# A two-block network on one core: the state space preparation moved behind the first mixer, its product turned, records on the SyncE queue, query weights split ahead, bias tables last

## The chip, the cores and the metric

The kernel runs on one core of one Trainium2 chip, as one launch. A core has five engines with instruction streams of their own: TensorE (PE; its weight loads are PEld), VectorE (DVE), ScalarE (ACT), GpSimd (POOL) and SyncE (SP, which here only issues DMAs). The metric is the device time of one execution in microseconds, as the median of several runs; lower is better.

## The reference

Two blocks for 256 tokens of width 1024, everything in fp32. The first block has two layers, each a hybrid mixer (gated linear attention, a short convolution and latent attention side by side, then an output projection) and cross-attention to a memory of 256 tokens. The second block has two layers of half-FFN, mixer, half-FFN; its first mixer is a state space layer (S5), its second a native sparse attention (NSA).

```python
x = first_block(x, mem, ...)                 # 2 x (hybrid mixer, memory cross-attention), final norm
for layer in range(2):                       # second block
    h = h + 0.5 * _swiglu(_rmsnorm(h, ffn1_norm[layer]), ffn1_w_in[layer], ffn1_w_out[layer])
    u = _rmsnorm(h, mix_norm[layer])
    h = h + (_s5_mixer(u, ...) if layer == 0 else _nsa_mixer(u, kv, w_qg, q_norm, w_o, rel_bias))
    h = h + 0.5 * _swiglu(_rmsnorm(h, ffn2_norm[layer]), ffn2_w_in[layer], ffn2_w_out[layer])
    if layer == 0:
        kv = _shared_kv(h, ...)              # keys and values of the three branches of NSA
```

The state space layer turns its parameters into a diagonal recurrence, which does not depend on the activations:

```python
def _s5_mixer(u, a_re, a_im, log_dt, b_re, b_im, c_re, c_im, d_skip, w_glu):
    dt = jnp.exp(log_dt)[:, None]
    ab_re, ab_im = exp(a_re * dt) * cos(a_im * dt), exp(a_re * dt) * sin(a_im * dt)
    bb = (ab - 1) / a * b                    # complex, per group, state and channel
    x = associative_scan(x[t] = ab * x[t - 1] + bb @ u[t])
    y = gelu(re(c @ x) + d_skip * u)
    return y * sigmoid(y @ w_glu)
```

NSA projects queries and gates from one weight matrix, takes relative position biases from a small table, and mixes compressed, selected and window attention.

## The kernel before, in words

Activations stay in SBUF. Every large product is made of three matmuls with 12-bit halves (`mm3` and the matmul helper, line 72): `xh*hi`, `xl*hi`, `xh*lo`. Each chunk of weights (1024 rows by 256 columns, 1 MB) is loaded by SyncE (line 143) into a ring of raw buffers; ScalarE rounds it to `hi` (line 155), VectorE subtracts to get `lo` (line 156), and PE uses both. One such chunk costs PE 48 matmuls for 256 tokens.

The stages in their order on the chip, with their times from the trace: mixer 0 (about 20 to 154 us), the memory keys and output projection of layer 0 (to 188), cross-attention 0 (to 245), mixer 1 (to 374), output projection 1 (to 410), cross-attention 1 (to 450), first half-FFN (to 661), S5 with its gate (to 750), half-FFN (to 945), shared keys and values (to 980), half-FFN (to 1187), NSA (to 1310), last half-FFN (to 1500).

Beside these runs a side generator, `self.side`. After each step of the main work `bg()` is called: it adds to an account a share of the PE time estimated since then (0.4 in the first block, 0.7 in the second, at most 10,000 ns) and takes steps of the generator until the account is used up. In the first block the generator is `startup`, which at its end goes on with `s5_prep`, the state space preparation. This first loads the small parameters, computes some 90 small VectorE operations of 128 by 32 elements (powers `pw`, factors `E`, parameters `prm`; helper line 1136), then one complex product on GpSimd, and then makes eight tiles, one after the other (`s5_prep_tile`). A tile is mostly a chain of GpSimd operations (helper line 60), with raw transposes, transposes of `X` and the product `pg` on PE (tile `pq`), copies by ScalarE, and three stores to DRAM, the record `stash`. What is left of the generator is drained in the last part of the first half-FFN's output (line 1330), where `s5_first` then loads record 0 back.

The program order of the source is not the order on an engine: a scheduler orders each engine's instructions by their dependences and estimated times. GpSimd alone keeps its program order (`InOrder`).

In S5, records 2 to 7 are read back by `s5_load`, each into a buffer that an earlier record leaves (`rec`, or `recw` in the ring of weights). In NSA a string of steps, `order`, gives the order of query chunks (R: projection; h, H: the heads' norms; T: transposes), gates (g), scores (S) and the rest.

## Time and profile before

| | |
|---|---|
| median of 3 runs | 1506.99 us (1506.6 to 1508.04) |
| the profiled execution | 1502.41 us, its span 1500.6 us |
| mean granted clock of TensorE | 0.976 |
| PE busy | 1434.1 us, 96% of the span |
| DVE, ACT, POOL busy | 1005.7, 740.0, 294.5 us |

The span is the time from the first to the last instruction of the profiled execution. Granted clock 1 is the full clock of TensorE, 0.5 the lower one. PE is busy nearly all the time, so that time can go or come in three ways: idle time of PE, stretches at the lower clock, and PE's own work.

### The profile page before, as it was taken

How to read it: one execution, taken by the hardware profiler on the slowest of the kernel's cores; microseconds unless marked ns; L12 is line 12 of the kernel's file. 1: busy time of each engine (PE TensorE's matmuls, PEld its weight loads, DVE VectorE, ACT ScalarE, POOL GpSimd, SP SyncE). 2: the span in 40 equal slices, each digit the busy share in tenths (PEclk: the TensorE clock that was granted, in tenths of full speed). 3: DMA queues.
4: the chain of work that ended last, by engine and by line, in shares of the span. 5: the costliest groups of instructions: out<-in, count | busy, mean ns of one | idle time of the engine just before them, and what ended most of it. 6: DMA issues, size and time to landing. Idle time of an engine off the chain costs nothing.

```text
span 1500.6 us, 28434 instructions
## 1 busy us (share of the span) xinstructions
PE 1434.1 (96%) x11767; PEld 1345.1 (90%) x11767; DVE 1005.7 (67%) x1782; ACT 740.0 (49%) x1248; POOL 294.5 (20%) x427
## 2 busy tenths in 40 slices
PE   8998999999999989988899999998999979999998
PEld 6897988889998989988799999898999967899987
DVE  6896756786767877448766665557765477666654
ACT  6745465645554444431354444446444477554442
POOL 2043531542547883010000000001000010000000
PEclk9998999999999999997899999999999999999999
DMA  7553554544635565695346556765555641155554
GB/s 195 148 145 116 183 169 122 155 145 154 203 115 175 198 211 197 200 322 177 131 141 196 181 182 195 210 179 152 170 181 193 195 127 43 57 169 192 177 195 138
DMA packets 240736, 252.69 MB, mean 168 GB/s; under 512 B 27825, under 2 KB 223255, under 8 KB 239712
## 3 DMA queue, kind: packets, MB, share of 16 engines
q1 hardware_dynamic: 234992, 226.75, 48.1%
q0 software_dynamic: 5328, 24.07, 4.8%
q8 instruction: 92, 1.51, 0.4%
q14 instruction: 36, 0.29, 0.1%
q10 hardware_dynamic: 288, 0.07, 0.0%
HBM read 235.40 MB, written 15.47 MB: 167 GB/s over the span
## 4 chain that ended last, share of the span: by engine, by line
PE 53%; issue 22%; DVE 8%; POOL 7%; DMA 6%; ACT 3%; POOLq 0%; SPq 0%; ACTq 0%; DVEq 0%
PE ps L72 44%; PE pb L72 5%; POOL pv L60 3%; DVE lo L156 3%; PE pq L72 2%; POOL pt L60 2%; DMA raw<-in_w_in_dram 2%; PE po L72 1%; POOL pX L60 1%; DMA raw<-in_ffn_w_in_dram 1%; ACT hi L155 1%; PE pb L76 1%; DMA stash<-pv 1%; DMA rec<-stash 1%; DMA memn<-in_mem_dram 1%
## 5 line engine op out<-in xcount | busy, mean ns | idle before, releaser
L156 DVE TENSOR_TENSOR lo<-raw,hi 128x1024 fp32r<-128x1024 f32 (+2 forms) x395 | 499.4, 1280 | 139.8 <-PE ps L72 83.9
L155 ACT ACTIVATE hi<-raw 128x1024 fp32r<-128x1024 f32 (+2 forms) x395 | 407.8, 1073 | 319.4 <-DMA raw<-in_ffn_w_in_dram 106.5
L72 PE MATMUL ps<-xh,hi 128*128 128x256 f32 x1848 | 524.1, 284 | 1.6 <-ACT xh L391 1.1
L72 PE MATMUL ps<-xh,lo 128*128 128x256 f32 x1848 | 521.1, 282 | 2.5 <-DVE lo L156 2.5
L72 PE MATMUL ps<-xl,hi 128*128 128x256 f32 x1848 | 521.5, 282 | 0.5 <-DVE xl L392 0.5
L72 PEld LDWEIGHTS ps<-xh,hi 128*128 128x128 f32 x1848 | 349.7, 189 | 7.7 <-issue 3.9
L72 PEld LDWEIGHTS ps<-xl,hi 128*128 128x128 f32 x1848 | 350.1, 189 | 5.5 <-issue 4.0
L72 PEld LDWEIGHTS ps<-xh,lo 128*128 128x128 f32 x1848 | 349.7, 189 | 5.7 <-DVE lo L156 4.0
L72 PE MATMUL ps<-gh,hi 128*128 128x256 f32 x576 | 163.0, 284 | 0.1
L72 PE MATMUL ps<-gl,hi 128*128 128x256 f32 x576 | 162.6, 283 | 0.0
L72 PE MATMUL ps<-gh,lo 128*128 128x256 f32 x576 | 162.4, 282 | 0.0
L72 PEld LDWEIGHTS ps<-gh,hi 128*128 128x128 f32 x576 | 109.5, 191 | 1.0 <-ACT gh L1474 0.3
L72 PEld LDWEIGHTS ps<-gl,hi 128*128 128x128 f32 x576 | 109.8, 191 | 0.2 <-issue 0.2
L72 PEld LDWEIGHTS ps<-gh,lo 128*128 128x128 f32 x576 | 109.7, 190 | 0.2
L1040 DVE TENSOR_TENSOR ab<-ps,rbf 128x512 f32<-128x512 f32 x66 | 45.5, 689 | 80.7 <-PE ps L72 77.2
L72 PE MATMUL ps<-L,hi 128*128 128x256 f32 (+1 forms) x384 | 73.4, 289 | 2.8 <-DVE e L549 2.8
L237 ACT ACTIVATE gh<-e 128x512 fp32r<-128x512 f32 x44 | 27.8, 631 | 87.7 <-DVE e L1047 87.7
L72 PEld LDWEIGHTS ps<-L,hi 128*128 128x128 f32 (+1 forms) x384 | 58.7, 184 | 3.8 <-DVE e L549 3.0
L72 PE MATMUL ps<-L,lo 128*128 128x256 f32 (+1 forms) x192 | 54.4, 285 | 0.0
L1045 ACT ACTIVATE e<-ab 128x512 f32<-128x512 f32 x44 | 27.8, 631 | 42.3 <-DVE ab L1040 42.2
L60 POOL TENSOR_TENSOR rkvs<-rkvsa,mhalf 128x2 f32<-128x2 f32 x1 | 0.7, 695 | 190.2 <-DVE rkvsa L371 190.2
L60 POOL TENSOR_TENSOR pX<-pt 64x256 f32<-64x256 f32 x32 | 37.3, 1167 | 2.2
(579 smaller groups left out, 2411.3 us busy)
## 6 DMA issues: line engine op xcount, KB each, us to landing
raw<-in_ffn_w_in_dram SPq DMA_DIRECT2D x88, 1024.0 KB, 5.2
raw<-in_ffn_w_out_dram SPq DMA_DIRECT2D x34, 1024.0 KB, 5.1
stash<-pv POOLq DMA_DIRECT2D x24, 512.0 KB, 4.3
raw<-in_w_in_dram SPq DMA_DIRECT2D x11, 1024.0 KB, 5.3
raw<-in_ffn_w_out_dram SPq DMA_DIRECT2D x12, 768.0 KB, 4.3
raw<-in_w_out_dram SPq DMA_DIRECT2D x8, 1024.0 KB, 5.7
raw<-in_w_in_dram SPq DMA_DIRECT2D x14, 512.0 KB, 5.4
rec<-stash POOLq DMA_DIRECT2D x4, 1536.0 KB, 9.0
```

The costliest lines, as they stand in the source:

```text
L60: return self.tc.keep_in_program_order(f(out, *a, **k))
L72: return self.engine.matmul(out, w, x, **k)
L76: return self.engine.transpose(out, x, ident)
L155: self.nc.scalar.activation(dst(hi), src(raw), AF.Copy)
L156: (engine or self.nc.vector).tensor_tensor(dst(lo), src(raw), dst(hi).bitcast(F32), op=SUB)
L237: self.nc.scalar.activation(hi, src, AF.Copy)
L1040: V.tensor_tensor(v[-1], p, rb2, op=MUL)
L1045: A.activation(th, v[0], AF.Tanh, scale=0.5)
```

## The change

Five edits in one:

1. The generator of the first block is now `startup` alone; `s5_prep` is chained behind it in layer 0 of the mixer, just before the memory keys and the output projection. Nothing of the preparation is issued before that.
2. In `s5_prep_tile` the product of `X` and `cb` is turned: before, `X` (128 columns) is the stationary operand and `cb` (32 columns) moves, 8 matmuls; now `cb` is stationary in four strips of 32 columns and `X` moves, 8 matmuls, then ScalarE copies the result to SBUF (`gw`, tile `pr`), and one PE transpose turns it back. A `yield` stands between.
3. `s5_load` issues all records on SyncE's queue.
4. In `shared_kv_rest` the bias tables come last.
5. In NSA the query weights are loaded and split one chunk ahead of their projection, and the string of steps is changed at its start.

```diff
@@ mixer
+        if l == 0:
+            self.side = chain(self.side, self.late)
         self.mem_k(l, take())
         self.out_proj(T["w_out"][l], xs, 256, self.add_h())
@@ first_block, startup and the main program
-                self.side = self.startup(self.side)
+                self.side = self.startup()
...
-        yield from then
+        yield
...
-    net.side = net.s5_prep()
+    net.late = net.s5_prep()
@@ s5_prep_tile
-        pg = self.ps("pq")[:, :P].rearrange("p (q c) -> p q c", q=4)
-        for q in range(4):
-            for c in range(2):
-                PE.matmul(pg[:, q, :], X[c][:, q * P:(q + 1) * P], cb[:, c, q].rearrange("p g h -> p (g h)"),
-                          start=c == 0, stop=c == 1)
+        pw_ = self.ps("pq")[:, :P]
+        for c in range(2):
+            for q in range(4):
+                PE.matmul(pw_[32 * q:32 * q + 32], cb[:, c, q].rearrange("p g h -> p (g h)"), X[c][:, q * P:(q + 1) * P],
+                          start=c == 0, stop=c == 1, skip_group_check=True)
+        gw = self.pz.tile([P, P], F32, name="pr", tag="pr", bufs=2)
+        A.activation(gw, pw_, AF.Copy)
+        yield
+        pg = self.ps("pq")[:, :P]
+        PE.transpose(pg, gw, self.ident)
+        pg = pg.rearrange("p (q c) -> p q c", q=4)
@@ s5_load
-        (engine or self.G).dma_start(t, self.stash[kt])
+        self.nc.sync.dma_start(t, self.stash[kt])
@@ shared_kv_rest: at its head, and at its end
-        yield from self.bias_tables()
...
+        yield from self.bias_tables()
@@ nsa (rows2 now takes the split weights)
+        wq = {0: self.wcols(W, 0, 256)}
...
-            p = self.rows2(W, 256 * j, x, "pq")
+            if j < 3:
+                wq[j + 1] = self.wcols(W, 256 * (j + 1), 256)
+            p = self.rows2(wq[j], x, "pq")
...
-        order = ("R0 h0 H0 R1 T0 h1 H1 R2 h2 g S0 S1 H2 R3 S2 T1 h3 H3 B0 c0 S3 t0 T2 S4 C0 T3 t1 V0 S5 B1 S6 S7 c1 "
+        order = ("R0 h0 R1 H0 h1 R2 T0 H1 h2 R3 g T1 S0 H2 S1 h3 S2 H3 B0 c0 S3 t0 T2 S4 C0 T3 t1 V0 S5 B1 S6 S7 c1 "
```

How the scheduler places this is seen at three places.

**VectorE.** Before, in mixer 0, the small operations of the preparation (`prm`, `pw`, `E`) stand among the weight splits (`lo`) and the attention's softmax (`as`, `ast`):

```order
L156 TENSOR_TENSOR lo<-raw,hi 128x1024
L1136 TENSOR_TENSOR E<-E,prm 128x32
L1136 TENSOR_TENSOR E<-E 128x32
L615 RECIPROCAL ast<-ast 128x2
L1173 TENSOR_SCALAR E<-E 128x32
L1136 TENSOR_TENSOR prm<-E 128x32
L1136 TENSOR_TENSOR E<-E 128x32
L1136 TENSOR_TENSOR prm<-E 128x32
L1136 TENSOR_TENSOR E<-E,prm 128x32
L618 TENSOR_SCALAR as<-as,ast 128x128
```

Now that place holds none of them, and they stand in the output projection of layer 0, among its weight splits and the memory keys (`kT`); there are 15 to 18 of them between the two `lo` of one chunk and those of the next:

```order
L421 SCALAR_TENSOR_TENSOR prm<-prm 128x32
L829 TENSOR_TENSOR kT<-ps,rmb 128x512
L421 SCALAR_TENSOR_TENSOR prm<-prm 128x32
L156 TENSOR_TENSOR lo<-raw,hi 128x1024
L421 SCALAR_TENSOR_TENSOR prm<-prm 128x32
L156 TENSOR_TENSOR lo<-raw,hi 128x1024
L421 SCALAR_TENSOR_TENSOR prm<-prm 128x32
L424 TENSOR_SCALAR prm<-prm 128x32
L1144 TENSOR_SCALAR prm<-prm 128x32
L418 TENSOR_SCALAR prm<-prm 128x32
L419 TENSOR_SCALAR prm<-prm 128x32
```

What moved are all of the small operations, some 90; GpSimd's part of the preparation follows behind them, and its first tile comes in cross-attention 0.

**TensorE.** Before, the product of one tile (here of tile 0, in mixer 0; its last three rows of eight) is followed directly by the main work; its result goes to ScalarE and VectorE, and PE has nothing more to do with it:

```order
L72 MATMUL pq<-pcb,pX_1359 128x32
L72 MATMUL pq<-pcb,pX_1217 128x32
L72 MATMUL pq<-pcb,pX_1359 128x32
L72 MATMUL pb<-kT,qT 128x128
L72 MATMUL ps<-xmh,hi 128x256
L72 MATMUL ps<-xml,hi 128x256
```

Now (here of tile 4) the eight matmuls have 32 columns, and the transpose of ScalarE's copy (`pr`) stands four matmuls behind them:

```order
L72 MATMUL ps<-xl,hi 128x256
L72 MATMUL pq<-pX_5296,pcb 32x128 x4
L72 MATMUL pq<-pX_5302,pcb 32x128 x4
L72 MATMUL ps<-xh,lo 128x256
L72 MATMUL ps<-xh,hi 128x256
L72 MATMUL ps<-xl,hi 128x256
L72 MATMUL ps<-xh,lo 128x256
L76 MATMUL pq<-ident,pr 128x128
L72 MATMUL ps<-xh,hi 128x256
```

So PE has a new instruction that waits for ScalarE. It stands behind 4 to 14 matmuls and transposes of other work in tiles 0, 1, 4, 6 and 7, and behind some 40 to 60 in tiles 2, 3 and 5.

**SyncE.** Before, its queue holds no record but the first two (`stash0`, `stash1`); the others are issued by GpSimd:

```order
L1349 DMA recw_7676<-stash1_653 128x3072
L143 DMA raw_7678<-in_s5_w_glu_2_dram 128x2x1024
L143 DMA raw_7781<-in_s5_w_glu_2_dram 128x2x1024
L1326 DMA ud1_7174<-u5_7171 512x1x256
L143 DMA raw_7970<-in_s5_w_glu_2_dram 128x2x1024
L143 DMA raw_8195<-in_s5_w_glu_2_dram 128x2x1024
L143 DMA raw_8677<-in_ffn2_w_in_2_dram 128x8x256
```

Now records 2 to 7 stand among the weights of the gate (`w_glu`) and of the next half-FFN (`ffn2_w_in`):

```order
L143 DMA raw_7710<-in_s5_w_glu_2_dram 128x2x1024
L143 DMA raw_7813<-in_s5_w_glu_2_dram 128x2x1024
L1357 DMA rec_7718<-stash2_1606 128x3072
L1334 DMA ud1_7142<-u5_7139 512x1x256
L1357 DMA rec_7912<-stash3_1607 128x3072
L143 DMA raw_8002<-in_s5_w_glu_2_dram 128x2x1024
L143 DMA raw_8227<-in_s5_w_glu_2_dram 128x2x1024
L1357 DMA recw_7996<-stash4_1608 128x3072
L1357 DMA rec_8113<-stash5_1609 128x3072
L143 DMA raw_8709<-in_ffn2_w_in_2_dram 128x8x256
L1357 DMA rec_8221<-stash6_1610 128x3072
L1357 DMA recw_8338<-stash7_1611 128x3072
```

Record 3 stands ahead of the last two loads of the gate's weights, and record 6 behind the first load of the next half-FFN.

The first half-FFN now holds the end of tile 3 and tiles 4 to 7 of the preparation, where before it held tiles 5 to 7. In NSA the rows of PE keep nearly their order; on VectorE the `lo` of the third and fourth query chunk now both stand ahead of the gates and the first scores.

## Rows read from the trace of the kernel before

**Rows 1.** The page, part 1: busy us (share of the span) xinstructions

```profile
PE 1434.1 (96%) x11767; PEld 1345.1 (90%) x11767; DVE 1005.7 (67%) x1782; ACT 740.0 (49%) x1248; POOL 294.5 (20%) x427
```

**Rows 2.** Stretches (us): each engine's busy time and records, granted clock, DMA share and rate

```profile
75.00:100.00 25.00, 24.66 (x189) 22.81 (x190) 24.99 (x116) 13.42 (x24) 5.72 (x5) 1.00 0.48 133
100.00:125.00 25.00, 18.99 (x125) 16.68 (x125) 20.50 (x30) 10.22 (x20) 20.17 (x23) 0.80 0.49 150
115.00:120.00 5.00, 1.94 (x5) 1.22 (x6) 2.46 (x5) 4.21 (x13) 2.85 (x5) 0.50 0.12 41
120.00:125.00 5.00, 5.00 (x18) 3.62 (x18) 3.05 (x7) 1.36 (x2) 4.31 (x5) 0.51 0.43 118
150.00:175.00 25.00, 24.86 (x207) 24.13 (x206) 21.92 (x29) 11.19 (x19) 19.53 (x29) 1.00 0.57 190
275.00:300.00 25.00, 24.07 (x163) 23.78 (x164) 18.49 (x23) 13.13 (x24) 9.34 (x11) 0.93 0.62 179
```

**Rows 3.** PE's waits, 45 to 130 us: total, times, longest

```profile
PE po L72 <- ACT asT L627: 6.0, 1, 6.0
```

**Rows 4.** Timeline of ACT from 112 us: start, duration, instruction, idle time and its releaser

```profile
113.46 2.00 ACT L155 ACTIVATE hi<-raw 128x1024 fp32r<-128x1024 f32 x2 [6.43 <-DMA raw<-in_w_in_dram]
...
117.52 0.87 ACT L627 ACTIVATE asT<-pb 128x384 f32<-128x384 f32 x2
```

**Rows 5.** Groups of VectorE: line 156 in 95:115 and 130:150, and one group of line 1136

```profile
L156 DVE TENSOR_TENSOR lo<-raw,hi 128x1024 fp32r<-128x1024 f32 x7 | 10.4, 1479 | 0.0
L156 DVE TENSOR_TENSOR lo<-raw,hi 128x1024 fp32r<-128x1024 f32 x3 | 3.6, 1215 | 0.0
L1136 DVE TENSOR_TENSOR prm<-prm x19: 180/185/502, 55.9 to 95.1; 128x32 f32<-128x32 f32 x19
```

**Rows 6.** Timeline of PE near 142 and near 740 us, and ScalarE's line 1287

```profile
141.19 1.04 PE L76 MATMUL pq<-ident,pX 128*128 128x128 f32 x8
142.48 1.97 PE L72 MATMUL pq<-pcb,pX 128*128 128x32 f32 x16
144.29 0.47 PE L72 MATMUL pb<-kT,qT 96*128 96x128 f32 x2
...
739.37 1.09 PE L72 MATMUL pq<-rs,recw 128*32 128x63 f32 x64
...
L1287 ACT ACTIVATE pt<-pq x8: 253/277/278, 144.6 to 564.0; 128x128 f32<-128x128 f32 x8
```

**Rows 7.** POOL and SP timelines, PE's waits from 450 to 662 us, one stretch

```profile
504.64 0.33 POOL L60 MEMSET pcb<- 128x256 f32 x1
...
542.99 0.33 POOL L60 MEMSET pcb<- 128x256 f32 x1
...
579.49 0.60 POOL L60 DMA_DIRECT2D stash<-pv  x1 [0.30 <-POOL pv L60]
645.40 1.12 SPq L1342 DMA_DIRECT2D pv<-stash  x1
PE pq L76 <- POOL pX L60: 3.7, 2, 3.1
550.00:560.00 10.00, 6.91 (x47) 6.67 (x46) 7.49 (x8) 6.25 (x8) 9.51 (x10) 0.83 0.76 256
```

**Rows 8.** PE's waits from 661 to 760 us, and POOL's timeline near 673 us

```profile
PE pb L72 <- DMA recw<-stash: 1.9, 2, 1.1
673.36 0.57 POOL L60 DMA_DIRECT2D rec<-stash  x1
```

**Rows 9.** PE's waits from 980 to 1060 us, and one stretch

```profile
PE pb L76 <- DVE e L1586: 3.6, 2, 2.5
1015.00:1020.00 5.00, 2.47 (x18) 2.30 (x19) 2.69 (x6) 3.87 (x7) 1.38 (x1) 0.91 0.64 210
```

**Rows 10.** PE's waits from 1187 to 1310 us, and one stretch

```profile
PE pb L76 <- DVE nst L1798: 2.8, 1, 2.8
1200.00:1235.00 35.00, 25.60 (x186) 21.91 (x186) 25.82 (x83) 26.65 (x63) 6.58 (x4) 0.99 0.38 114
```

More of the change, by code (lines that the diff above doesn't have):

```diff
@@ L198, in rows, with rows2 @@
         return p
-    def rows2(self, W, c0, x, tag="ps"):
+    def rows2(self, w, x, tag="ps"):
         p = self.ps(tag).rearrange("p (t c) -> p t c", t=2)
-        w = self.wcols(W, c0, 256)
         for k in range(KD):
@@ L838, in mem_v @@
         def mem_v(i):
-            p = self.rows2(T["mem_wv"][l], 256 * i, self.xmem)
+            p = self.rows2(self.wcols(T["mem_wv"][l], 256 * i, 256), self.xmem)
             for t in range(2):
@@ L969, in first_consts, with startup @@
             self.am.append(a)
-    def startup(self, then):
+    def startup(self):
         yield
@@ L1343, in s5_first, with s5_load @@
             self.rec = {0: rec0}
-            self.s5_load(1, self.win, 0, self.nc.sync)
-    def s5_load(self, kt, pool, bufs, engine=None):
+            self.s5_load(1, self.win, 0)
+    def s5_load(self, kt, pool, bufs):
         t = self.t("rec", [P, 3072], bufs=bufs, pool=pool) if bufs else self.t("recw", [P, 3072], pool=self.win)
-        (engine or self.G).dma_start(t, self.stash[kt])
+        self.nc.sync.dma_start(t, self.stash[kt])
         self.rec[kt] = [t[:, 1024 * i:1024 * i + 1024] for i in range(3)]
```

## The prediction

> **What bounds the kernel now.** I read the busy times first: PE is busy 1434.1 us of a span of 1500.6, 96%, and every other engine has room on the mean, DVE at 67% the least [rows 1]. So nothing that merely lightens DVE, ACT or POOL shortens the run; only an edit that ends a wait of PE, lifts its clock, or takes work from PE does. I then went through the stretches for those places. The worst ahead of S5 is the end of mixer 0: in 100 to 125 us PE works 18.99 of 25 us, and in 115 to 120 and 120 to 125 the granted clock is 0.50 and 0.51, the lower level of 1.2 GHz, after PE had fallen idle [rows 2]. The list of waits names one of 6.0 us there, for `asT` of ScalarE [rows 3]. ScalarE's timeline says why `asT` is late: it first waits 6.43 us for a weight load (`raw`), then does two splits, then reaches `asT` at 117.52 [rows 4]. The load is late because the raw buffers come free behind VectorE's `lo`, and VectorE is busy 24.99 of 25 us in 75 to 100, with 116 records [rows 2]. Many of these are small operations of the preparation; the largest group is 19 of 185 ns, the last at 95.1 us [rows 5]. When POOL is busy (20.17 of 25 us in 100 to 125 [rows 2]), `lo` takes 1479 ns on the mean, against 1215 later [rows 5]. So the preparation is what fills VectorE, and the stall is a late consequence of it.
>
> **The change, part by part.**
>
> *Preparation moved: what leaves mixer 0.* The loss there is 25 - 18.99 = 6.0 us idle, and 1.94 + 5.00 us of work at half clock [rows 2], which at full clock takes half: 3.5 us. Together 9.5. About 90 operations at 0.2 us (185 ns [rows 5], with the pitch somewhat less) give VectorE 16 to 18 us back in a stretch of 40, and POOL falls silent there. I do not take all of 9.5: the same place of mixer 1, which never held that set-up, still has 0.9 us idle and a clock of 0.93 in 275 to 300 [rows 2], together up to 0.9 + 0.07 x 25 = 2.7. I take -8; bounds -9.5 and -4 (half of the stall stays, if the weight load is late for another reason).
>
> *What arrives in the output projection.* VectorE has 21.92 us of work in 150 to 175 now, beside a POOL busy 19.53 [rows 2]. In that row 207 records of PE take 24.86 us, 0.12 each, so a chunk of 48 is 5.8 us. On VectorE a chunk is two `lo` at 1.2 us, some 16 small operations (3 us) and one or two steps on the residual (1 us): 6.5. Over five chunks it falls behind by 3 us, while three weight buffers run ahead, and POOL's first tile is not there to slow `lo`. I take +1; bounds 0 and +4.
>
> *The turned product.* Before, 16 records take from 142.48 to 144.29, 1.81 us a tile, of which their 32 moving columns explain little: the 128 columns of each stationary operand do, for eight transposes with as many columns take 1.04 us, 0.13 each [rows 6]. After, the strips are 32 columns. The nearest row is S5's, also 32-column strips, 63 columns moving: 64 records in 1.09 us, 17 ns each [rows 6]. With twice the columns that is 34 ns, 0.55 us for 16; the upper bound is 128 columns at half the price of 256, 0.06 us, 0.94 for 16. I take 0.6, and 0.13 for the transpose: 1.81 - 0.73 = 1.08 us a tile, 8.6 for eight. Against it stands the wait for ScalarE's copy. Its like, line 1287, begins 0.3 us after the product's end and takes 0.28 [rows 6], so PE could go on some 0.7 us after it, and a split ahead of the copy adds up to 1 us. Tiles 2, 3 and 5 have 40 and more matmuls as cover (5 us); tiles 0, 4, 6 and 7 only 0.5 to 0.8, tile 1 some 1.5. That is 0.2 to 1 us for each of four tiles; I take 2.6. Net -6; bounds -9 (no waits) and +1 (0.94 for the strips, 1.5 us in each of five tiles).
>
> The Trainium skill ("TensorE: Matmul & The Clock Gate", section "LDWEIGHTS (loading the stationary operand)") says that a weight load costs time by its columns alone, P / 1.2 ns; by it 16 loads are 1.71 us before and 0.43 after, an estimate by that page, so that the gain would be 1.15 us a tile, 0.6 more over eight. The 1.81 us of the tile [rows 6] agree with the first; S5's 17 ns a record is below the page's 27 ns, so by the row strips cost less still.
>
> *The first half-FFN.* It holds four whole tiles in place of three. POOL needs 38.4 us a tile (504.64 to 542.99) and ends with the store at 579.49; PE waits 3.7 us for `pX`, and in 550 to 560 it works 6.91 of 10 us at clock 0.83 [rows 7]. In the order, raw transposes of successive tiles stood 288 matmuls apart (34 us and 3.5 of the preparation's own PE work, 37), so PE came early; now the gaps are 382, 288 and 336 (48, 37 and 43 us), so at one gap only. I take -2 for one wait less with its clock; bounds -4 and +4 (each of four tiles waits as those two did). Record 0 is fetched at 645.40 [rows 7]. The drain stands so that POOL ends near 640 by this pace, 188 + 8 x 56. The cover is thin, 5 us ahead of the fetch, but S5 itself begins only at 661, 16 us behind it.
>
> *Records on SyncE.* PE waits 1.9 us for `recw` [rows 8]. Record 3 no longer stands behind POOL's work (673.36 [rows 8]) and can leave near 667, at the price that the gate's last weights stand behind it. The issue itself (0.57 us [rows 8]) is off PE's path. -1.5; bounds -4 and +2.
>
> The Trainium skill ("DMA: Bandwidth & Descriptors", section "Issuing engines are not separate DMA queues") holds that DMAs of all issuers share the same 16 engines, so that another issuer saves only issue time. By it this term is 0 and the sum -19.5; no run here shows yet which holds.
>
> *Bias tables last.* PE waits 3.6 us for `e` of the heads' norm, and 1015 to 1020 has 2.47 of 5 us busy [rows 9]: the keys' norms stand behind the tables' work. They now come first, and the tables have all of the half-FFN to 1187 us as cover. -2.5; bounds -6 and +2 (the same small operations collide with PE elsewhere).
>
> *NSA.* 35 - 25.60 = 9.4 us idle in 1200 to 1235, with a wait of 2.8 for `nst` as the longest [rows 10]. The split ahead helps the projections R2 and R3, but the orders show PE's rows almost unchanged, and both `lo` now stand ahead of the gates and scores on VectorE. I take -2; bounds -9 and +2.
>
> **The sum.** -8 + 1 - 6 - 2 - 1.5 - 2.5 - 2 = -21. Against the profiled execution's 1502.4 us this is 1481.4; the median lies 4.6 above that execution, so for the median 1507.0 - 21 = **1486 us**.
>
> **The rivals.**
>
> *The stall only moves.* For it speaks that VectorE gets the same 17 us in the output projection, where it was 88% busy; against it, that PE waits there for few of its results. It gives half of mixer 0's gain back: +4 and the output projection at +4, sum -14, 1493 us.
>
> *The product's gain is lost to the copy.* For: the new transpose stands 4 matmuls behind in tile 4 and PE keeps its order. Against: ScalarE is busy 49%. Sum -15 to -20, within the likeliest case's range.
>
> *NSA or the bias tables pay in full.* -9 and -6 in place of -2 and -2.5: sum -31, 1476 us. For: the idle time is there [rows 9, 10]. Against: it is a chain of several short waits.
>
> *Slower: GpSimd becomes the bound of the first half-FFN.* PE runs in its fixed order and waits for `pX` of each of four tiles, and S5 begins late for record 0. With POOL at 38.4 us against a mean gap of 43 this does not happen; it does if a tile takes over 49 us: then each tile costs 6 us with its clock, four 24, and the change ends above zero: 1512 us. The tile in the row stays 10 us below that.
>
> *No change.* If ScalarE's late load in mixer 0 had another cause (+8) and the copy ate the product's gain (+6), -21 becomes -7; for none, NSA and the tables would have to fail too.
>
> **Chances.** Gain of 12 to 30 us: 0.62. Stall only moves, gain 4 to 12: 0.14. More than 30: 0.09. Within 0.2% (3 us, about what a measurement of this kernel can tell from no change): 0.06. Slower: 0.09. So faster is 0.85, same 0.06, slower 0.09. The likeliest case's range is 1477 to 1495; for 8 in 10 I reach to the second rival's and third's times: 1470 to 1500.
>
> **What would show it.** In mixer 0 the wait for `asT` is gone, VectorE falls under 20 of 25 us in 75 to 100, and the clock is 1.0 in 115 to 125. The output projection keeps PE at 24 of 25 us. The product's 16 records take 0.6 us, and PE's waits for `pr` sum to 2 to 4 us. POOL's last store lies before 645 us. `recw` is waited for under 1 us, and the wait for `e` at 1015 is gone. I am wrong if PE waits for POOL in each tile of the half-FFN, if record 0 comes after 670 us, or if the idle time of mixer 0 returns in 154 to 245.

## The result, and the profile after

The changed kernel takes 1491.70 us (median of 4 runs, 1488.95 to 1491.89) against 1506.80 of the kernel before beside it (4 runs, 1504.76 to 1508.04): a ratio of 0.990, with a 95% interval of 0.988 to 0.991, so 15.1 us less. The profiled execution took 1491.53 us, its span 1489.8, with a mean granted clock of 0.981. It lies 10.9 us below the profiled execution of before, which itself lay 4.4 below its median. The stage lengths below add up to 10.8 of these 10.9; the other 4 us between the medians stand in no stage.

Part 1 of the page after, to set beside [rows 1]:

```profile
PE 1421.8 (95%) x11775; PEld 1329.9 (89%) x11775; DVE 1004.0 (67%) x1782; ACT 738.3 (50%) x1256; POOL 294.2 (20%) x421
```

PE is busy 12.3 us less, in a span 10.8 us shorter, so its idle time did not shrink: 66.5 us before, 68.0 after. What went is time at the lower clock and PE's own work; the idle time has changed its place. The stretches show where (columns as in [rows 2]; the last two lie 4 and 9 us earlier than those of before, since the program is 3.6 and 8.4 us ahead there):

```profile
75.00:100.00 25.00, 24.88 (x194) 23.04 (x193) 16.30 (x38) 12.37 (x25) 0.00 (x0) 1.00 0.50 143
100.00:125.00 25.00, 24.99 (x198) 22.16 (x197) 18.01 (x42) 12.51 (x26) 0.00 (x0) 1.00 0.40 127
150.00:175.00 25.00, 25.00 (x213) 25.00 (x212) 23.29 (x103) 12.74 (x19) 0.00 (x0) 1.00 0.52 170
182.00:190.00 8.00, 0.50 (x4) 0.19 (x4) 2.61 (x2) 4.98 (x14) 7.74 (x11) 0.76 0.33 123
190.00:200.00 10.00, 10.00 (x69) 8.32 (x66) 2.70 (x5) 4.27 (x7) 9.50 (x12) 0.85 0.32 107
450.00:648.00 198.00, 186.89 (x1597) 182.84 (x1596) 142.27 (x177) 89.71 (x141) 137.67 (x182) 0.98 0.64 208
1011.00:1016.00 5.00, 4.28 (x35) 3.83 (x33) 0.74 (x5) 4.82 (x14) 0.54 (x1) 1.00 0.85 200
1191.00:1226.00 35.00, 28.42 (x189) 24.49 (x188) 23.20 (x76) 23.26 (x59) 6.58 (x4) 0.90 0.23 73
```

Mixer 0 is whole: 24.99 of 25 us in 100 to 125 at clock 1.00, VectorE down from 24.99 to 16.30 in 75 to 100, the wait for `asT` of [rows 3] gone. The output projection keeps PE full (25.00 of 25 in 150 to 175) though VectorE now has 103 operations there. But 182 to 190 us, the begin of cross-attention 0, has PE busy 0.50 of 8 us, and the next 10 us run at 0.85 of the clock: a new stall, with POOL busy 7.74 of those 8 us.

PE's waits of after over the whole run (total, times, longest) have these at their head:

```profile
PE pb L72 <- ACT sq L351: 9.2, 3, 7.6
PE pq L72 <- ACT pv L1276: 8.2, 4, 3.6
PE ps L72 <- DVE lo L156: 7.5, 7, 2.4
```

To price stages, I read the last addition to the residual (`hT`) in each from VectorE's timeline; a stage's length is the distance of two such rows. Of before, the first and the last of output projection 0:

```profile
165.58 0.69 DVE L231 TENSOR_TENSOR hT<-ps,hT 128x512 f32<-128x512 f32 x1 [1.40 <-PE ps L72]
...
182.62 0.69 DVE L231 TENSOR_TENSOR hT<-ps,hT 128x512 f32<-128x512 f32 x1 [1.93 <-PE ps L72]
```

and of after:

```profile
151.83 0.69 DVE L230 TENSOR_TENSOR hT<-ps,hT 128x512 f32<-128x512 f32 x1 [0.93 <-PE ps L72]
...
170.71 0.68 DVE L230 TENSOR_TENSOR hT<-ps,hT 128x512 f32<-128x512 f32 x1
```

So the first of them comes 13.75 us earlier and the last 11.91. All stages, in us, of the two kernels and of the experiments below (op: mixer with its output projection; x: cross-attention; ff: half-FFN; kv: shared keys and values):

```
                  op 0    x 0    op 1    x 1   ff 1     S5   ff 2  kv+ff    NSA
before          182.62  52.57  161.83  52.35  211.89  90.82  190.23  243.96  121.29
after           170.71  60.58  162.38  52.11  215.09  87.44  190.44  239.12  118.88
e1_late_only    169.83  60.95  160.34  57.27  216.05  90.33  188.68  243.16  121.11
e2_early_memset 172.09  62.66  165.87  52.06  216.47  87.53  190.24  238.80  118.92
e3_old_product  169.93  61.49  160.42  55.37  217.47  88.43  190.25  238.13  117.86
e4_psum_pb      170.49  61.49  161.49  52.53  213.85  90.14  190.24  238.93  118.82
e5_no_late      181.69  52.29  171.55  50.96  216.74  87.18  188.90  238.27  118.30
e6_gate         169.90  53.19  172.25  58.22  222.64  87.54  189.77  240.02  117.55
e7_gate_share   170.56  53.95  172.16  56.36  222.94  94.94  190.23  238.14  119.25
e8_rec_pool     170.41  61.67  162.89  51.80  215.97  93.36  190.41  238.20  119.70
e9_gate_tiles   169.82  52.66  172.99  50.13  222.77  87.86  190.21  238.68  121.31
e10_bias_first  171.30  62.27  161.83  51.97  214.01  87.36  190.42  243.70  118.19
e11_nsa_old     172.56  61.84  163.09  52.22  214.60  91.67  189.99  240.16  121.35
e12_one_tile    169.00  66.23  175.21  47.86  191.04  87.06  188.66  239.42  119.01
```

A stage whose code is the same still moves by a few us from one profile to another (op 0 of e11_nsa_old is 172.56 against 170.71, its S5 91.67 against 87.44), so a single difference is good to some 2 us, and some miss by 4. Groups of kernels tell more: cross-attention 0 is 52.3 to 52.6 where the preparation begins in mixer 0 and 60.6 to 66.2 where it begins behind the mixer and nothing holds it back.

**The new stall, read backwards.** TensorE's timeline of after at 189.50 us shows what it waited for, the squares `sq` for the norm of cross-attention 0:

```profile
189.50 1.07 PE L72 MATMUL pb<-sq,ones 128*32 128x256 f32 x4 [7.62 <-ACT sq L351]
```

ScalarE's timeline of after says why the squares are late. They stand behind the copies into `pcb` (lines 1253, 1254: the block matrix of the preparation's tile 0), and the first of these waits 6.89 us for POOL:

```profile
177.21 0.82 ACT L844 ACTIVATE qT<-ps,rm 128x256 f32<-128x256 f32 x2
...
184.92 0.22 ACT L1253 ACTIVATE pcb<-pq 64x64 f32<-64x64 f32 x1 [6.89 <-POOL pcb L60]
...
186.31 2.00 ACT L155 ACTIVATE hi<-raw 128x1024 fp32r<-128x1024 f32 x2
...
188.83 1.14 ACT L351 ACTIVATE sq<-hT 128x512 f32<-128x512 f32 x2
```

And POOL's timeline of after says why `pcb` is late. The copy needs nothing but POOL's clearing of the buffer (line 60, MEMSET), which takes 0.31 us, but stands in program order behind the complex product of the preparation (`bb`, `pv`), which begins only when VectorE's `prm` are there:

```profile
175.78 1.07 POOL L60 TENSOR_TENSOR bb<-pX,prm 128x512 f32<-128x512 f32 x1 [47.27 <-DVE prm L1138]
...
182.16 2.48 POOL L60 TENSOR_TENSOR bb<-bb,pv 128x512 f32<-128x512 f32 x2
184.58 0.31 POOL L60 MEMSET pcb<- 128x256 f32 x1
...
197.00 0.71 POOL L60 TENSOR_TENSOR rx<-rxa,mhalf 128x2 f32<-128x2 f32 x1
```

So none of these steps computes anything for `sq`: two engines that execute in order each hold a step of the main work behind a step of the preparation. The last row is the second one of that kind: `rx`, the power of the norm, has its input (`rxa`) since 194.5 and runs at 197.00 between two operations of tile 0.

One sentence ahead of the prediction has to be narrowed: what moved is the preparation's computing. SyncE still fetches its parameters early, the first at 31.8 us:

```profile
L1129 SPq DMA_DIRECT2D pX<-in_s_b_re_dram x1: 424/424/424, 31.8 to 31.8; - x1
```

**Where the product's gain goes.** PE's groups on tile `pq` of after in 450 to 650 us (instructions | busy us, mean ns | idle time ahead of them and its releaser):

```profile
L76 PE MATMUL pq<-ident,pX 128*128 128x128 f32 x32 | 4.4, 274 | 0.9 <-POOL pX L60 0.9
L72 PE MATMUL pq<-pX,pcb 128*32 128x128 f32 x64 | 3.0, 313 | 6.5 <-ACT pv L1276 6.5
L76 PE MATMUL pq<-ident,pr 128*128 128x128 f32 x10 | 2.6, 307 | 0.0
```

and of before in 450 to 661 us:

```profile
L72 PE MATMUL pq<-pcb,pX 128*128 128x32 f32 x48 | 5.6, 271 | 0.0
```

A tile's product cost 5.6/3 = 1.9 us of PE and costs 3.0/4 = 0.75, or less: in TensorE's timeline of after one takes 0.57 us to the next start (the one that follows the longest wait runs at 0.52 of the clock and takes 1.0). But 6.5 us of idle time now stand ahead of these matmuls. The timeline:

```profile
474.74 1.03 PE L76 MATMUL pq<-ident,pX 128*128 128x128 f32 x8
479.65 1.08 PE L72 MATMUL pq<-pX,pcb 128*32 128x128 f32 x16 [3.63 <-ACT pv L1276]
481.68 0.41 PE L76 MATMUL pq<-ident,pr 128*128 128x128 f32 x1
...
516.85 0.65 PE L72 MATMUL pq<-pX,pcb 128*32 128x128 f32 x16
517.42 0.39 PE L72 MATMUL ps<-xh,lo 128*128 128x256 f32 x1
```

The transposes of `X` at 474.74 fill both buffers of the PSUM pool `pq`. The turned product needs one of them, and so has to wait until ScalarE has copied one out (`pv`, line 1276), behind the two splits of a weight chunk, which themselves wait 1.08 us for their load, as ScalarE's timeline of after shows:

```profile
476.97 2.00 ACT L155 ACTIVATE hi<-raw 128x1024 fp32r<-128x1024 f32 x2 [1.08 <-DMA raw<-in_ffn_w_in_dram]
479.00 1.09 ACT L1276 ACTIVATE pv<-pq 128x512 f32<-128x512 f32 x2
```

### The profile page after: what moved, and what is told of

Same layout as the page of the kernel before. It is cut to its first block, busy times and chain, and to the rows that moved or that the text cites. A ratio compares the mean times of both kernels' runs of the same rounds, so it can differ in the third digit from the quotient of the medians.

```text
span 1489.8 us, 28460 instructions
## 1 busy us (share of the span) xinstructions
PE 1421.8 (95%) x11775; PEld 1329.9 (89%) x11775; DVE 1004.0 (67%) x1782; ACT 738.3 (50%) x1256; POOL 294.2 (20%) x421
## 4 chain that ended last, share of the span: by engine, by line
PE 60%; DVE 10%; issue 9%; POOL 8%; DMA 6%; ACT 5%; SPq 0%; POOLq 0%; ACTq 0%; DVEq 0%
PE ps L72 51%; PE pb L72 5%; DVE lo L156 4%; POOL pv L60 3%; POOL pt L60 2%; PE pq L72 2%; ACT hi L155 2%; DMA raw<-in_w_in_dram 2%; POOL pX L60 1%; PE po L72 1%; DMA raw<-in_w_out_dram 1%; DMA stash<-pv 1%; DMA raw<-in_ffn_w_out_dram 1%; PE pb L76 1%; DVE xl L391 1%
## 5 line engine op out<-in xcount | busy, mean ns | idle before, releaser
L72 PEld LDWEIGHTS ps<-L,lo 128*128 128x128 f32 (+1 forms) x192 | 35.4, 185 | 2.8 <-DVE lo L156 2.7
```

Of the source, the lines that this page charges most:

```text
L72: return self.engine.matmul(out, w, x, **k)
```

## The experiments

Two theories stood at the outset for cross-attention 0. The *queue*: the stall is made by steps of the main work that stand behind the preparation's on ScalarE and POOL. The rival, *VectorE*: the 90 small operations in the output projection make VectorE late, as they had in mixer 0, and the stall is that lateness. The other edits were undone one at a time, to set their stage beside the prediction's term. Times are medians; each ratio is to the kernel before on the same chip, with its 95% interval. The expectations count from 1491.7 us, beside which the kernel before took 1506.80; beside the experiments it took 1503.47 to 1506.90, so the whole times are best compared by the ratios (0.9897 for the change), and the stages by the table.

**The first edit alone.** The kernel before with edit 1 of the five and nothing else:

```diff
+        if l == 0:
+            self.side = chain(self.side, self.late)
         self.mem_k(l, take())
...
-                self.side = self.startup(self.side)
+                self.side = self.startup()
```

> The kernel before with the first edit alone: the preparation chained behind mixer 0, everything else as before. Theory: mixer 0 gives about 13 us, of which the start of cross-attention 0 takes 8 to 10 back in one wait of PE for ScalarE's squares (7.6 us in the changed kernel), and the four whole tiles in the first half-FFN with the old product take some 3 more, so the time is 1502 to 1506 us (before 1506.8). Rival (the preparation is worth its full stall, 8 us and more): 1493 to 1499 us.

1506.95 us, ratio 0.9997 (0.9975 to 1.0018): nothing, to within some 3 us. PE's waits of this kernel in 125 to 262 us have the stall at their head:

```profile
PE pb L72 <- ACT sq L352: 7.3, 1, 7.3
```

Mixer 0 gives 12.8 us, cross-attention 0 takes back 8.4 at once, cross-attention 1 and the half-FFN 9.1 more by the table. So the stall belongs to this edit, not to the turned product, and the whole gain of the change lies in what is done beside it or with it. The stage lengths came as the theory had them, but for the half-FFN and cross-attention 1, which lost 9 us where 3 were expected.

**The clearing early.** Takes the first of the two queues out: POOL clears `pcb` ahead of the complex product.

```diff
+        cb = self.pt("pcb", 1)
+        G.memset(cb[:, :256], 0.0)
         cmul([h16(bb[:, i, :]) for i in range(2)], [h16(t) for t in bn], zb,
```

> The changed kernel with one instruction moved: GpSimd clears tile 0's buffer pcb ahead of its complex product, not behind it. Theory (ScalarE stands at its copy into pcb for 6.9 us, waiting for that clearing, and PE's squares stand behind the copy): the wait of 7.6 us falls under 2 us and the time to 1483 to 1486 us (changed kernel 1491.7). Rival (VectorE's small operations in the output projection make everything late there): the wait stays at 5 us or more and the time within 2 us of 1491.7.

1499.13 us, ratio 0.9948 (0.9928 to 0.9968), and cross-attention 0 still 62.66. PE's waits of this kernel in 154 to 250 us:

```profile
PE pb L72 <- ACT sg L869: 5.8, 1, 5.8
PE pb L72 <- ACT sq L351: 1.6, 1, 1.6
```

The wait for `sq` falls from 7.6 to 1.6, as the queue has it, and another of 5.8 takes its place. POOL's and VectorE's timelines of this kernel show the second queue, by itself now:

```profile
189.82 0.16 DVE L370 TENSOR_SCALAR rxa<-pb 128x2 f32<-128x2 f32 x1 [2.88 <-PE pb L72]
199.61 0.62 DVE L896 TENSOR_SCALAR rxs<-rx 128x2 f32<-128x2 f32 x1 [9.62 <-POOL rx L60]
...
198.86 0.71 POOL L60 TENSOR_TENSOR rx<-rxa,mhalf 128x2 f32<-128x2 f32 x1
```

`rx` has its input at 190.0 and runs at 198.86, behind tile 0. One queue opened is no gain while the other one holds the same path. The wait fell as expected, the time did not: by its profile this kernel takes 7.8 us more than after, 2.1 of them in cross-attention 0 and 3.5 in mixer 1. The rival fails too, since the wait for `sq` goes with the clearing while VectorE's operations stay.

**Gates.** Two kernels hold the preparation back until the program has issued `rx` of cross-attention 0, one ahead of the complex product:

```diff
+        while not self.go:
+            yield True
         bb = self.pz.tile([P, 2, 512], F32, name="bb", tag="bb", bufs=1)
...
         r = self.rpow(self.sumsq(self.hT, KD, "pb"), D, 2, "rx")
+        self.go = True
```

> The changed kernel with a gate: the small VectorE operations stay in output projection 0, but GpSimd's part (complex product and tiles) may start only behind the power rx of cross-attention 0's norm. Theory (ScalarE's copies into pcb and GpSimd's rx both stand in order behind tile 0, and either alone holds the norm back): neither wait remains, cross-attention 0 ends 6 to 8 us earlier than in the changed kernel, and the time is 1483 to 1488 us if the last tile, some 15 us later, still ends ahead of record 0's fetch. Rival (VectorE's operations in the output projection delay the norm): a wait of over 4 us stays at the start of cross-attention 0, time 1490 to 1494. Second rival (the tiles come too late): record 0 or S5 waits, over 1492 us.

and one ahead of the first tile:

```diff
+        while not self.go:
+            yield True
         for kt in range(KD):
             yield from self.s5_prep_tile(kt, v, pw, bb, E)
```

> The changed kernel with the gate further on: VectorE's small operations and GpSimd's complex product may run in output projection 0, only the tiles wait for rx; the last tile is placed where the changed kernel has it. Theory (ScalarE's copies into pcb and GpSimd's rx, in order behind tile 0, are what holds the norm of cross-attention 0): that stage ends 6 to 8 us earlier than in the changed kernel; what is kept of it at the end depends on which of the main work's small GpSimd operations fall behind a tile later, so 1483 to 1494 us. Rival (VectorE's load): a wait of over 4 us for the squares stays at the start of cross-attention 0.

Cross-attention 0 falls to 53.19 and 52.66, the length of before, with VectorE's 90 operations still in the output projection. PE's waits of the second kernel in 160 to 260 us have no more of the stall than this:

```profile
PE pb L72 <- ACT sq L352: 1.6, 1, 1.6
```

So the queue makes the stall, not VectorE, whose rival asked for a wait of over 4 us. Not all of it is gone: PE is idle 5.44 and 4.16 us in this stage, against 10.06 in after and 0.83 in before, and a part of the shorter stage is tile 0's product, which now comes later. VectorE stays a link of the chain, as POOL's complex product cannot begin ahead of `prm`; whether an earlier `prm` would clear the path was not tried. But the totals are 1503.39 us, ratio 0.9967 (0.9946 to 0.9988), and 1506.80 us, ratio 1.0014 (1.0001 to 1.0027), both above the changed kernel's, where 1483 to 1494 had been expected. The time is lost again in mixer 1 (172 to 173 against 162.38) and in the half-FFN (222.7 against 215.09), which now holds the products of five tiles in place of four. The second rival of the first gate has the time, but not its reason, that S5 waits for late records: S5 takes 87.54. TensorE's timeline of the second of them:

```profile
271.22 0.90 PE L76 MATMUL pq<-ident,pX 128*128 128x128 f32 x3 [10.27 <-POOL pX L60]
```

The transposes of a tile's `X` stand there in PE's order while POOL is still in the tile before, and PE waited 10.27 us, as much as mixer 1 loses in this kernel. For the first gate's mixer 1 the cause was not followed.

**A gate and a larger share.** To make up for the held back time, the first gate with 0.5 in place of 0.4 of PE's time for the side generator:

```diff
-        self.at, self.owed, self.share = 0, 0, 0.4
+        self.at, self.owed, self.share = 0, 0, 0.5
```

> The same gate, and in the first block the side work may take 0.5 of PE's estimated time in place of 0.4, so that the tiles come earlier again than in the gate alone. Theory: as with the gate, 1482 to 1488 us, with the last tile before that of the changed kernel. Rival (more tiles in mixer 1 and cross-attention 1 cost there what they save in the half-FFN): mixer 1 and cross-attention 1 lose 3 to 6 us against the gate alone, 1488 to 1493.

1506.43 us, ratio 1.0009 (0.9989 to 1.0028). Cross-attention 0 is 53.95, but mixer 1 takes 172.16 and the half-FFN 222.94, so the time expected of it, 1482 to 1493, is missed as well. S5 takes 94.94, with a wait of 4.0 us for `recw` though SyncE issues the records. This kernel's profile lies 6.9 us above its median. No better place for the tiles was found this way.

**The preparation where it was.** Edit 1 undone, the other four kept:

```diff
-        if l == 0:
-            self.side = chain(self.side, self.late)
...
-                self.side = self.startup()
+                self.side = self.startup(self.side)
```

> The changed kernel with the first edit alone undone: the preparation follows the start-up loads in mixer 0 again, all other edits stay. Theory (the first edit is worth nothing by itself, since what mixer 0 gains is lost at the start of cross-attention 0 and in the first half-FFN): within 4 us of the changed kernel, 1488 to 1496 us, with the wait for asT in mixer 0 back and the 7.6 us for sq gone. Rival (the first edit carries the gain, as the prediction's largest term had it): 1499 to 1504 us.

1503.65 us, ratio 0.9985 (0.9971 to 0.9999), so the theory fails and the rival's time came in, though not for the rival's reason alone. The wait for `asT` is back (6.1 us) and the stall of cross-attention 0 gone, as in before, and these two nearly cancel (mixer 0 is 10.98 us longer than in after, cross-attention 0 8.29 shorter). The rest is for the most part mixer 1, which takes 171.55, 9 us more than in after and 9.7 more than in before. PE's two longest waits there, in 230 to 410 us:

```profile
PE pb L76 <- DVE on L702: 3.1, 2, 2.6
PE ps L72 <- DVE e L591: 2.3, 1, 2.3
```

The first of them goes back to POOL. Timelines of VectorE and POOL of this kernel:

```profile
354.28 0.17 DVE L370 TENSOR_SCALAR rga<-gms 128x8 f32<-128x8 f32 x1
...
358.49 1.82 POOL L60 TENSOR_TENSOR pt<-pcb,pw 128x256 f32<-128x256 f32 x2 [16.41 <-ACT pcb L1251]
362.85 1.66 POOL L60 TENSOR_TENSOR rg<-rga,mhalf 128x8 f32<-128x8 f32 x1
```

The input of `rg` is there at 354.45, but POOL, in order, sits 16.41 us in front of a step of the preparation that waits for ScalarE, and `rg` runs at 362.85. In after, the like operation ran as soon as its input came. It is the stall of cross-attention 0 once more, at another place: 3.1 us of waiting and, with a clock of 0.91 in 360 to 380 us, some 1.8 behind it, about half of the 9. The second wait does not run over a step of the preparation: `e` stands behind ScalarE's `qT`, and ScalarE had waited 2.39 us for a weight load ahead of that. In 304 to 312 us the granted clock is 0.50, another 4 us; what lowered it was not followed. So what edit 1 is worth depends on what the tiles and loads happen to hold up elsewhere. Alone it is worth nothing; beside the others some 9 us by the two profiles and 13 by the ratios.

**The old product,** edit 2 undone:

```diff
-        pw_ = self.ps("pq")[:, :P]
...
+                PE.matmul(pg[:, q, :], X[c][:, q * P:(q + 1) * P], cb[:, c, q].rearrange("p g h -> p (g h)"),
+                          start=c == 0, stop=c == 1)
```

> The changed kernel with the second edit undone: X is stationary again, no copy, no transpose. Theory (the turned product saves 1.0 us of PE work a tile, but PE now waits for ScalarE to empty a bank, 8.2 us in four waits, because the next user of the bank comes sooner): these waits fall to 2 to 4 us, the product's work grows by 8, and the time is 1493 to 1497 us. Rival (the turned product is worth its full 8 us, the waits for the bank stay): 1499 to 1501 us. Second rival (it is worth nothing): within 1 us of 1491.7.

1498.39 us, ratio 0.9937 (0.9912 to 0.9962). PE's waits for `pv` are gone, and one for POOL's `pX` stands there (PE's waits of this kernel in 450 to 670 us):

```profile
PE pq L76 <- POOL pX L60: 3.4, 2, 2.8
```

From the end of cross-attention 0 to that of the half-FFN it takes 433.3 us against 429.6 of after: the turned product is worth 3.7 us there, net, which is the theory's size; the ratio gives 6.0 for the whole run.

**The product in another PSUM pool,** so that it needs no buffer of `pq`:

```diff
-        pw_ = self.ps("pq")[:, :P]
+        pw_ = self.ps("pb")[:, :P]
```

> The changed kernel with the turned product's result in the PSUM buffers named pb in place of those named pq, so that it need not wait until ScalarE has copied the transposes of X out of pq. Theory: the four waits for pv (8.2 us in all) go and the time falls by 4 to 7 us, to 1485 to 1488. Rival (the wait is only passed on, to the transpose of the copy or to the attention's users of pb): waits for pr or pb of about the same sum, time within 2 us of 1491.7.

1494.98 us, ratio 0.9907 (0.9872 to 0.9941). The wait for `pv` vanishes, and the next instruction inherits it, the transpose of the copy (PE's waits in 450 to 670 us):

```profile
PE pq L76 <- ACT pr L1286: 6.6, 3, 3.6
```

ScalarE is what is late, behind its weight splits; a free buffer only lets PE meet that one step further on. This is the rival, in its waits and, by the ratio, in its time.

**Records on GpSimd,** edit 3 undone:

```diff
-        self.nc.sync.dma_start(t, self.stash[kt])
+        (engine or self.G).dma_start(t, self.stash[kt])
```

> The changed kernel with the third edit undone: records 2 to 7 are issued by GpSimd again. Theory: S5 gained 3.4 us by stages between the profiles of before and after, and the records are the only edit that touches it, so S5 takes 3 to 4 us more and the time is 1494 to 1496 us. Rival (issuer does not matter, S5's gain came from where it started): S5 within 1 us of the changed kernel's.

1499.13 us, ratio 0.9955 (0.9932 to 0.9978). S5 takes 93.36 in place of 87.44, 5.9 us more where 3 to 4 were expected, and the wait of [rows 8] is back (PE's waits in 665 to 760 us):

```profile
PE pb L72 <- DMA recw<-stash: 3.1, 2, 2.0
PE pb L72 <- DMA rec<-stash: 0.4, 1, 0.4
```

**Bias tables first,** edit 4 undone:

```diff
+        yield from self.bias_tables()
         for br in range(2):
             for t in range(2):
...
-        yield from self.bias_tables()
```

> The changed kernel with the fourth edit undone: bias tables ahead of the keys' norms. Theory: between the ends of the two half-FFNs the changed kernel gained 4.8 us on the kernel before, all of it by this edit, so that stage takes 4 to 5.5 us more, the wait for e (3.6 us) is back, and the time is 1495 to 1498 us. Rival (the gain came from where the side work stood after S5): within 2 us of 1491.7.

1495.05 us, ratio 0.9947 (0.9930 to 0.9964). As expected, the stage takes 243.70 in place of 239.12, and the wait of [rows 9] is back (PE's waits in 980 to 1190 us):

```profile
PE pb L76 <- DVE e L1594: 4.2, 3, 2.7
```

**NSA as it was,** edit 5 undone, the weights and the string:

```diff
-            if j < 3:
-                wq[j + 1] = self.wcols(W, 256 * (j + 1), 256)
-            p = self.rows2(wq[j], x, "pq")
+            p = self.rows2(self.wcols(W, 256 * j, 256), x, "pq")
...
-        order = ("R0 h0 R1 H0 h1 R2 T0 H1 h2 R3 g T1 S0 H2 S1 h3 S2 H3 B0 c0 S3 t0 T2 S4 C0 T3 t1 V0 S5 B1 S6 S7 c1 "
+        order = ("R0 h0 H0 R1 T0 h1 H1 R2 h2 g S0 S1 H2 R3 S2 T1 h3 H3 B0 c0 S3 t0 T2 S4 C0 T3 t1 V0 S5 B1 S6 S7 c1 "
```

> The changed kernel with the fifth edit undone: query weights split when their projection comes, the old string of steps. Theory: NSA gained 2.4 us on the kernel before by stages, so 1493.5 to 1495 us. Rival (that gain followed from the bias tables' new place): within 1 us of 1491.7.

1496.79 us, ratio 0.9960 (0.9947 to 0.9973). NSA takes 121.35 in place of 118.88, the 2.4 us of the theory, with the wait of [rows 10] back (PE's waits in 1185 to 1320 us):

```profile
PE pb L76 <- DVE nst L1806: 2.8, 1, 2.8
```

**One tile only.** To price the preparation as a whole: tiles 1 to 7 are left out, and tile 0 is stored as all eight records.

```diff
-        for kt in range(KD):
-            yield from self.s5_prep_tile(kt, v, pw, bb, E)
+        yield from self.s5_prep_tile(0, v, pw, bb, E)
...
-        out = lambda i, t: self.G.dma_start(dst[:, 1024 * i:1024 * i + 1024], t)
+        out = lambda i, t: [self.G.dma_start(d[:, 1024 * i:1024 * i + 1024], t) for d in self.stash]
```

> The changed kernel without tiles 1 to 7 of the preparation: tile 0 is made as before and stored as all eight records, so S5 computes with one tile's parameters. Theory (what the preparation costs is not only PE's own work for it, some 1.9 us a tile, 13 for seven, but as much again in waits of the main work behind it on ScalarE, VectorE and GpSimd): cross-attention 0 keeps its 7.6 us, and from there to the end of the first half-FFN 24 to 30 us are saved, so 1462 to 1468 us. Rival (the waits there are the main work's own): 12 to 16 us saved, 1476 to 1480.

1482.10 us, ratio 0.9859 (0.9845 to 0.9874). The half-FFN takes 191.04 in place of 215.09. One stretch of it:

```profile
460.00:648.00 188.00, 186.90 (x1605) 184.95 (x1605) 115.06 (x134) 84.36 (x97) 2.34 (x2) 1.00 0.61 204
```

PE is idle 1.1 us of 188 there, in after 11.1 of 198. So four tiles and the end of a fifth cost the half-FFN 24 us: 10.0 of PE's own work (4.4 + 3.0 + 2.6 in the groups above), 10 of idle time, and 0.02 of the clock over 187 us, about 3.7. That is the theory's account, but only of this one stage. Cross-attention 0 and mixer 1 are longer here (66.23 and 175.21), and over the whole stretch that the expectation names, from cross-attention 0 to the end of the half-FFN, 15.5 us are saved (414.11 in place of 429.58), which is the rival's figure; the whole time lies above what either had. Why mixer 1 is longer is not shown; tile 0's 24 stores stand bunched on POOL, 4.3 us for eight, and 5.7 us of PE's waits there are for VectorE's `e`. So what the preparation costs as a whole stays open. No kernel that does all of the work was faster than the changed one, by the ratios.

## Why the prediction was right, and where it was not

The direction and the range held; the gain was 15.1 us where 21 had been forecast, and the 1491.7 us lie nearer to the rival "the stall only moves" (1493) than to the forecast (1486). Most of the single checks came in: `asT`, VectorE under 20 of 25 us, the clock at 1.00, the output projection at 25.00 of 25, 0.57 us for 16 records, POOL's last store at 625.90 (before 645), no wait for `recw`, and no more than 0.8 us of the waits for `e`. Two did not: the waits for `pr`, and "the idle time of mixer 0 returns in 154 to 245", which the text had named as a sign of its being wrong. By its own steps, with what the two profiles measured:

- *Preparation moved, -8.* The first residual addition comes 13.75 us earlier. 3.4 of that are the work of tile 0 on PE (2.0 for the product and 1.0 for the transposes in [rows 6], 0.4 for two transposes of raw parameters) that now stands later, so the stall itself gave 10.3: all of the 9.5 that were counted, where a rest of 1.5 had been held back. The reading of [rows 4] left one thing out: between the two splits and `asT` ScalarE made eight copies of the preparation's tile 0, all of them between 115.37 and 117.50 us, so that the queue on ScalarE that decides cross-attention 0 was to be seen in before:

```profile
115.37 0.20 ACT L1251 ACTIVATE pcb<-pq 64x64 f32<-64x64 f32 x1
```

How much of the stall was VectorE's and how much ScalarE's or POOL's part of the preparation was not separated, since all of it left together.
- *What arrives in the output projection, +1.* **This is the step that failed.** PE is full there, as predicted. But the step priced the moved work on VectorE alone and to the end of the output projection alone; ScalarE's and POOL's part of tile 0, which comes right behind, was not priced at all. Over the output projection and cross-attention 0 the change loses 13.75 - 3.90 = 9.85 us (3.90 is what is left at the end of cross-attention 0), of which 7.5 are idle time in 182 to 190 and 1.5 the clock in 190 to 200. So mixer 0's gain of 10.3 is all but gone, and e1_late_only, which has this edit alone, gains nothing over the whole run. The Trainium skill ("PSUM — Partial Sum Buffer", section "Engine vs sequencer instructions") has the rule that was needed, that the queues of ScalarE, VectorE and GpSimd are strict FIFO; the trace agrees: on ScalarE the squares stood behind a copy that waited 6.89 us, and on POOL `rg` of e5_no_late ran 8.4 us after its input was there. The rival "the stall only moves" saw that this could be, with half the price and for VectorE, which by the two gates is not what makes most of it.
- *The turned product, -6.* Gross it is as computed. Its wait was looked for at the copy `pr`, 2.6 us; the list of waits has none there. It stands one step earlier, at the PSUM buffer: 8.2 us in the whole run for `pv`, in four waits. Net, -3.7 by e3_old_product.
- *First half-FFN, -2.* From the end of cross-attention 0 to that of the half-FFN the kernel with the old product takes 7.2 us more than before. 3.4 are the tile's work from mixer 0, so this term is +3.8, at the edge of its bounds; 3.0 of it stand in cross-attention 1 (55.37 against 52.35), so it is not the wait of each tile that had been feared. In after itself PE's idle time in the half-FFN is 11.1 us (198 - 186.89): the wait for `pX` did shrink (3.7 [rows 7] to 0.9), but `pv` with 6.5 more than took its place. What four tiles cost in all is shown by e12_one_tile.
- *Records, -1.5.* S5 is 3.4 us shorter, and e8_rec_pool, which undoes the edit, 5.9 longer than after. Record 3 leaves at 666.54 instead of 673.36 [rows 8], at the same begin of S5 (661.3 before, 660.9 after):

```profile
666.54 0.63 SPq L1357 DMA_DIRECT2D rec<-stash  x1
```

The Trainium skill ("DMA: Bandwidth & Descriptors", section "Issuing engines are not separate DMA queues") gave this term as 0. What the other engine changes is when the issue is reached, behind whose work it stands: 6.8 us earlier for record 3. The records also land sooner after their issue (`rec` 6.9 us at the median against 9.0 in before), and which of the two brings the gain was not separated. The measurement decides for the term. The wait for `recw` is in all three kernels in which GpSimd issues (1.8 to 3.1 us, S5 90.3 to 93.4), but also in two of the eleven in which SyncE does (1.3 in e4_psum_pb, 4.0 in e7_gate_share), so the edit makes it rarer and does not rule it out.
- *Bias tables, -2.5.* -4.8; e10_bias_first gives back 4.6. The stretch of the wait for `e` [rows 9] now has 4.28 of 5 us busy instead of 2.47; only the size was too small.
- *NSA, -2.* -2.4; e11_nsa_old gives back 2.5. The size was right, the place is not shown: the stretch of [rows 10] has 6.6 us idle in place of 9.4, but its clock is 0.90 in place of 0.99, so that it holds as much work as before (28.42 x 0.90 = 25.6 against 25.60 x 0.99 = 25.3).

For the sixteen strips of the turned product the Trainium skill ("TensorE: Matmul & The Clock Gate", section "LDWEIGHTS (loading the stationary operand)") led to an estimate of 0.43 us, the row of S5 to 0.55; the trace has 0.57, and decides for the row.

The sum of the terms as measured: -10.3 + 9.85 - 3.7 + 3.8 - 3.4 - 4.8 - 2.4 + 0.2 (half-FFN 2) = -10.75. That this agrees, to 0.1, with the difference of the two profiled executions is no test of the terms, as they are cut from the same stage lengths. The first two edits, forecast at -15, come to -0.35 in these profiles (-10.3 + 9.85 - 3.7 + 3.8), and edits 3 to 5 gave 10.6 in place of 6. That the total fell inside the range is therefore in good part luck.

**What stays open.** The kernels with one edit undone lose more by their medians than by the stage that the edit concerns: by the ratios to before 6 to 13 us each, 45 in all, where the whole change brings 15. Part of that is shown (e5_no_late: new waits in mixer 1; e11_nsa_old: S5 is 4.2 us longer in its profile, with the same 11.8 us of idle time of PE but at 0.80 in place of 0.83 of the clock, without a cause that was found). The rest may be the edits' effects on each other through the scheduler, or the spread between chips: the changed kernel was not run again beside them, so the sizes above go by stage lengths, good to some 2 us. And that a combined repair of both queues, clearing and `rx`, would bring cross-attention 0 back without cost was not tried.

## What to carry to other kernels

Work that is moved off a crowded stretch has to be priced on every engine that it uses, and above all on those that run in program order: not how long it lasts counts but which step of the main work stands behind its first waiting instruction (here 0.31 us of clearing behind other work held PE up for 7.6). When a wait is removed, ask what the same consumer, or the next one, waits for at that moment, for otherwise it is only handed on, as the PSUM buffer's was to the copy, and the clearing's to `rx`. And undo each edit by itself and do it by itself: edit 1 is worth nothing alone and 9 to 13 us in company.

## What was not expected of the hardware

The cost of the strips goes by the moving columns: 64 records of 63 columns took 1.09 us [rows 6], 16 of 128 columns 0.57, which is 0.27 and 0.28 ns a column, both at a granted clock of 1.00. These are two rows; no other width was run.

A stall costs more than its length here. Behind the one that ended at 189.50 us, with PE busy 10.00 of 10 us again, the granted clock is 0.85, a mean of both levels (2.4 and 1.2 GHz): 1.5 us on top of 7.5. In e9_gate_tiles the 10 us in which PE stood still are granted 0.57, near the lower level:

```profile
261.00:271.00 10.00, 0.00 (x0) 0.00 (x0) 5.14 (x7) 1.91 (x9) 9.33 (x13) 0.57 0.62 196
```

POOL's `bb<-bb,pv` takes 1.24 us a piece in after (2 in 2.48) and 2.23 in e2_early_memset (2 in 4.47), for the same shapes. VectorE stands idle beside the first, from 180.3 to 187.4 us; beside the second it makes two `lo`, from 183.1 to 186.9, which take 1.9 us each where [rows 5] have 1.2. So in these rows both engines are slower when they work side by side; no run was made to separate it.
